# Memory keys and values inside the last attention head, sums of the normed x on VectorE, all gates in the pair stream

## The chip, the core and the metric

The kernel runs on one core of a Trainium2 chip. The core has TensorE (PE: matrix products, with a separate path for weight loads, PEld), VectorE (DVE), ScalarE (ACT), GpSimd (POOL) and SyncE (SP), each with its own instruction stream, and 16 DMA engines that move data between DRAM and the core's SBUF. The metric is the device time of one execution in microseconds (us); less is better. Three executions of the kernel before took 2409.5, 2413.11 and 2413.56 us; the median is 2413.11.

## The reference, cut to what matters

One layer of a streaming encoder runs on 1024 prompt tokens and 64 sample tokens (1088 in all), width 1024, in float32. One input projection makes the queries, keys and values of eight attention heads, the two inputs of a recurrent branch, the queries of a memory attention and three sets of gates. Beside it, 256 memory tokens are normed and turned into keys and values:

```python
def memory_kv(mem, g, wk, wv, k_norm_g):
    b, n, _ = mem.shape
    m = rms_norm(mem, g)
    k = rms_norm((m @ wk).reshape(b, n, MEM_HEADS, MEM_HEAD_DIM), k_norm_g)
    v = (m @ wv).reshape(b, n, MEM_HEADS, MEM_HEAD_DIM)
    return k.transpose(0, 2, 1, 3), v.transpose(0, 2, 1, 3)

def layer(x, past_k, past_v, conv_buf, h0, mem_k, mem_v, lw):
    xn = rms_norm(x, lw["norm_mix_g"])
    proj = xn @ lw["w_in"]
    # q_sb, k_sb, v_sb (8 heads x 128), x_lru, g_lru, q_mem (4 x 256), gates (3 x 1024)
    o_sb = stick_breaking_attention(q_sb, k_all, v_all, q_pos, k_pos)
    # o_lru: convolution, gated recurrence; o_mem: attention of q_mem over mem_k, mem_v
    g = jax.nn.sigmoid(gates + lw["b_merge"]).reshape(b, t, N_BRANCH, D_MODEL)
    merged = (g[:, :, 0] * (o_sb @ lw["w_br_sb"]) + g[:, :, 1] * (o_lru @ lw["w_br_lru"])
              + g[:, :, 2] * (o_mem @ lw["w_br_mem"]))
    x = x + merged @ lw["w_out"]
    # then a gated feed-forward block with its own norm
```

The memory keys and values of the prompt are outputs of the kernel and also operands of the memory attention, which comes much later.

## The kernel before, in words

**Products.** Every operand of a product is split into a high and a low half (`split`, L71 and L72: ScalarE casts the high half, VectorE or, where `l_eng=G` is given, GpSimd subtracts it to get the low half), and each product of tiles is three TensorE products (`mm3`, L99 to L101). Tokens lie along the free dimension in four chunks of 272. A weight of 1024 rows by 128 columns is loaded as one raw 128x1024 tile (three buffers, tag `raw`) and split into `wh` and `wl` (two buffers each); its load is issued on ScalarE's queue (L79).

**Stages in order.** The input is normed and transposed into operands B11, B12, B21, B22 (0 to about 40 us). Then come eight attention heads, then the memory keys and values (L791 to L842), then a stream of paired projections which fills the recurrent stage and the memory attention, then the branch outputs, the output projection and the feed-forward block.

**Fillers.** Attention alone does not fill TensorE: it waits for ScalarE and VectorE. So other products are issued between its parts. `Bulk` holds a generator; `bulk.run(n)` issues `n` steps of it at that place of the program. In the attention stage the generator is `bulk.steps(sb_stream())`: tile after tile of plain projections, three tiles (V, Q, K) for each head, each of 4 chunks x 8 steps, so 96 steps a head, one step three products of 128x272. While head `h` is computed, the tiles of head `h + 1` are issued. The last head has no next one; there the stream has four plain tiles of gates (`gate_tile`, `GATES_SB = 4`), 128 steps.

**The sums.** The later stream computes pairs of projections by seven products of sums of operands instead of eight products. It needs four sums per pair of row blocks: T3, T1, T2, T4, kept in DRAM. `x_sums` (L604 to L633) makes them from the normed x: 32 operations of 128x544 on GpSimd, in three buffers (`xq`). They are issued in a generator that the program advances between the steps of the heads; since nothing but the normed x is needed, most of them are done at the start.

**Order.** A scheduler (the tile framework) places each instruction by its place in the program and the priorities given; `high_priority` moves the emptying of a PSUM bank ahead. Each engine runs its own list in order. A buffer of a pool is reused when the last reader of its former content is done, and places in the pools of a later stage overlap those of an earlier one in SBUF: the pool `bt` (operands T2, T4, T1 of the stream and four spare places) lies where the attention pool `sb` was, while T3 lies in the places of B12.

**The memory section.** Two memory tiles are normed (L650), transposed in eight steps (L804) and scaled into `mTh` and `mTl`; then 16 halves (four heads, K and V, two halves each) of 8 x 3 products of 128x256 follow, each with its own weight; `mem_out` transposes the result back to tokens, norms the keys and stores. The key norm's factors are spread over the partitions by GpSimd (L796).

**The stream.** `pair_stream` (L738) issues 22 pairs, each seven operations of 24 products in 14 steps, 308 steps: 8 pairs of the recurrent inputs, 4 of the memory queries and 10 of the gates. The recurrent stage takes 14 + 8 x 23 of them, the memory attention 6 + 4 x 28; together that is 316, so the stream before runs out in the last memory head. If steps remain, they run by themselves behind it.

Of the kernel before, what the change touches and what calls it, by code (L numbers as in the profile page):

```python
# [2 lines left out]

# [6 lines left out]
F32 = mybir.dt.float32  # L10
# [7 lines left out]
P = 128  # L18
# [7 lines left out]
H = 8  # L26
# [22 lines left out]
def kernel(ctx: ExitStack, tc: tile.TileContext, x_prompt, x_sample, mem_prompt, cache_sb_k, cache_sb_v,  # L49
# [35 lines left out]
    GATES_SB = 4  # L85
# [183 lines left out]

    def gate_tile(b, f):  # L270

        def ev(ci, s, n, p):
            st = wpl.tile([P, HT], F32, tag="stg", name="gst", bufs=4)
            V.tensor_copy(st[:, :n], p)
            ST.dma_start(g_scr[b][f][:, s:s + n], st[:, :n])

        c0 = CGATE + b * D + f * P
        return (lambda: load_w(w_in[0, :, c0:c0 + P], f"wg{b}{f}", l_eng=G)), ev, []
# [39 lines left out]
    with ExitStack() as c1:  # L318
# [263 lines left out]
        heads, outs = {}, {}  # L582

        def sb_stream():
            tiles = []
            for h in range(H):
                tiles += sb_tiles(h)
            return tiles + [gate_tile(0, f) for f in range(GATES_SB)]

        bulk.gen = bulk.steps(sb_stream())  # L590
# [13 lines left out]
        def x_sums():  # L604

            for i in range(KT // 2):
                def quarter(k, half):
                    q = sb.tile([P, HT], F32, tag="xq", name=f"xq{k}{half}", bufs=3)
                    u = xq(k, half)
                    G.tensor_add(q, f32(u[:, 0]), f32(u[:, 1]))  # L610
                    return q
# [6 lines left out]
                G.tensor_sub(t3, t3, t1)  # L618
# [4 lines left out]
                G.tensor_sub(t1, t1, t2)  # L623
                ST.dma_start(s_scr[i]["T1"], t1)
                yield
                G.tensor_add(t2, t2, t3)
# [4 lines left out]
                G.tensor_sub(t4, t4, t2)  # L631
# [12 lines left out]
        mts = []  # L644
        for t in range(2):
            mt = o_tile(f"mt{t}")[:, :D]
            ST.dma_start(mt, mem_prompt[0, t * P:(t + 1) * P, :])
            junk = sb.tile([P, D], F32, tag=("ah", "al")[t], name="junk")
            S.activation(junk, mt, AF.Square, accum_out=ssx[:, t:t + 1])
            V.tensor_scalar(mt, mt, rstd(sb, ssx[:, t:t + 1], D, "rx"), None, op0=ALU.mult)  # L650
            mts.append(mt)
# [86 lines left out]
    def pair_stream(pairs, last):  # L738
# [14 lines left out]
        for i, (_, dst, _) in enumerate(pairs):  # L753
# [10 lines left out]
               f"wg{b}{j}_") for b in range(3) for j in range(NI) if b or 2 * j >= GATES_SB]  # L764

    with ExitStack() as c2:
# [23 lines left out]

        gkb = mk.tile([P, MHD], F32, name="gkb", bufs=1)
        gkr = mk.tile([1, MHD], F32, name="gkr", bufs=1)
        LD.dma_start(gkr, k_norm_g)
        G.partition_broadcast(gkb, gkr)  # L796
        mTh = mk.tile([P, KT, MEM], F32R, name="mTh", bufs=1)
        mTl = mk.tile([P, KT, MEM], F32R, name="mTl", bufs=1)

        def mem_norm():  # L800
            for k in range(KT):
                p = ps.tile([P, 512], F32, tag="gt", name="mtp", bufs=3)
                for t in range(2):
                    TE.transpose(p[:, t * P:(t + 1) * P], mts[t][:, k * P:(k + 1) * P], ident)  # L804
                gk = prm[:, PNE + k:PNE + k + 1]
                S.activation(mTh[:, k, :], p[:, :MEM], AF.Copy, scale=gk)
                V.scalar_tensor_tensor(mTl[:, k, :], p[:, :MEM], gk, f32(mTh[:, k, :]),
                                       op0=ALU.mult, op1=ALU.subtract)

        def mem_half(u, c, kf):  # L810

            c0 = (u // 2) * MHD + c * P
            wh, wl = load_w((w_mem_v if u % 2 else w_mem_k)[0, :, c0:c0 + P], f"wm{u}{c}")
            p = psm.tile([P, 512], F32, tag="mm", name="mmk")
            for k in range(KT):
                mm3(p[:, :MEM], wh[:, k, :], wl[:, k, :], mTh[:, k, :], mTl[:, k, :], k == 0, k == KT - 1)
            V.tensor_copy(kf[:, c, :], p[:, :MEM])

        def mem_out(u, kf):
            m, is_v = u // 2, u % 2  # L820
            p = ps.tile([P, 2, MHD], F32, tag="gt", name="mkt", bufs=3)
            for t in range(2):
                for c in range(2):
                    TE.transpose(p[:, t, c * P:(c + 1) * P], kf[:, c, t * P:(t + 1) * P], ident)
            ko = wpl.tile([P, HT], F32, tag="stg", name="ko", bufs=4)[:, :512].rearrange("p (t d) -> p t d", t=2)
            if is_v:
                V.tensor_copy(ko, p)
            else:
                ss = mk.tile([P, 2], F32, tag="ssk", name="ssk")
                for t in range(2):  # L830
                    S.activation(ko[:, t, :], p[:, t, :], AF.Square, accum_out=ss[:, t:t + 1])
                r = rstd(mk, ss, MHD, "rk")
                for t in range(2):
                    V.scalar_tensor_tensor(ko[:, t, :], p[:, t, :], r[:, t:t + 1], gkb, op0=ALU.mult, op1=ALU.mult)
            ST.dma_start((o_mv if is_v else o_mk)[0, 0, m].rearrange("(t p) d -> p t d", p=P), ko)

        mem_norm()
# [525 lines left out]
```

## Time and profile before

| | |
|---|---|
| runs | 2409.5, 2413.11, 2413.56 us; median 2413.11 |
| profiled execution | 2409.07 us, span 2407.3 us |
| TensorE busy | 2275.7 us of the span (95%), granted clock 0.981 |
| VectorE, ScalarE, GpSimd busy | 1613.1, 1204.9, 762.5 us |
| first score of head 0, of the last head | 88.32, 538.54 us |
| first memory transpose | 612.47 us |
| first product of the stream | 682.68 us |

The profile shows one execution. Its time of 2409.07 us is that of the whole execution, 1.8 us more than the span of the instructions. In rows of the stage view, an engine's busy time is followed by the number of its instructions in brackets. In rows of groups, `out<-in` are the names of tiles, then come shapes, the count, the busy time and the mean of one in ns, and behind the bar the idle time ahead of them with what ended most of it. In rows of single instructions the first two numbers are the start and the duration in us, and brackets at the end hold the idle time ahead with its releaser.

### The profile page before, as it was taken

The page shows a single profiled execution, that of the slowest core. Times are in us where ns is not written, and L with a number is a line of the kernel's source. Part 1 is how long each engine was busy: PE and PEld are TensorE (multiplying, and loading weights), DVE is VectorE, ACT ScalarE, POOL GpSimd, SP SyncE. Part 2 cuts the span into 40 slices and gives each one's busy share as a digit, 9 for nine tenths or more (in the row PEclk, how much of TensorE's full clock was granted, in tenths as well). Part 3 has the DMA queues.
Part 4 walks back from the last instruction along what each step waited for, and adds up shares of the span by engine and source line. Part 5 has one row for each costly group of instructions (what it writes and reads, how often), then busy time and mean ns, then how long its engine had stood idle before and what let it go on. Part 6 is the DMA issues. An engine that isn't in the chain of part 4 may idle for free.

```text
span 2407.3 us, 44757 instructions
## 1 busy us (share of the span) xinstructions
PE 2275.7 (95%) x17477; PEld 2210.0 (92%) x17477; DVE 1613.1 (67%) x2843; ACT 1204.9 (50%) x2449; POOL 762.5 (32%) x735
## 2 busy tenths in 40 slices
PE   6899999999899999999999999898999999999998
PEld 6788888888899999999999998888999999999998
DVE  4365656566767777766667758678766666677884
ACT  4355555555447565645566645466433333353553
POOL 5623232322002232111112265735334334340110
PEclk9899999999899999999999999999999999999999
DMA  4212121212744444434456645233223233263543
GB/s 158 89 51 76 53 76 51 68 42 94 224 132 139 142 156 149 140 124 129 132 185 215 221 128 193 78 121 102 95 86 109 95 100 101 86 219 117 172 138 88
DMA packets 329738, 293.26 MB, mean 122 GB/s; under 512 B 19491, under 2 KB 261366, under 8 KB 329526
## 3 DMA queue, kind: packets, MB, share of 16 engines
q1 hardware_dynamic: 283288, 267.26, 34.3%
q10 hardware_dynamic: 46238, 23.15, 3.3%
q8 instruction: 137, 2.24, 0.4%
q14 instruction: 75, 0.61, 0.1%
HBM read 194.34 MB, written 95.99 MB: 121 GB/s over the span
## 4 chain that ended last, share of the span: by engine, by line
PE 53%; DVE 9%; POOL 4%; DMA 4%; ACT 2%; issue 2%; SPq 0%; ACTq 0%; POOLq 0%; DVEq 0%
PE sw L192 46%; POOL swt L1129 1%; POOL mg L1133 1%; DMA sig<-g 1%; PE ssq L967 1%; DVE xc L872 1%; PE mmk L101 1%; DMA xT<-sT 1%; DVE x2T L72 1%; PE mmk L100 1%; PE mmk L99 1%; DVE x1T L72 0%; DVE h1T L72 0%; DVE xgT L72 0%; PE avm L99 0%
## 5 line engine op out<-in xcount | busy, mean ns | idle before, releaser
L202 ACT COPY swt<-sw 128x272 f32<-128x272 f32 x432 | 164.3, 385 | 217.1 <-PE sw L192 215.1
L1253 POOL TENSOR_TENSOR u<-u,R 128x272 f32<-128x272 f32 x66 | 65.8, 998 | 171.2 <-DVE u L1252 164.0
L462 DVE SCALAR_TENSOR_TENSOR e<-z,e 128x384 f32<-128x384 f32 (+4 forms) x96 | 51.1, 551 | 92.6 <-ACT e L460 92.3
L192 PE MATMUL sw<-xT,wg_S 128*128 128x272 f32 x720 | 101.6, 293 | 0.0
L192 PEld LDWEIGHTS sw<-xT,wg_S 128*128 128x128 f32 x720 | 94.8, 192 | 0.0
L463 DVE TENSOR_TENSOR_SCAN e<-ones,e 128x128 f32<-128x128 f32 (+3 forms) x64 | 92.4, 1451 | 0.6
L748 DVE TENSOR_TENSOR swt<-sw,swt 128x272 f32<-128x272 f32 x132 | 56.6, 434 | 49.5 <-PE sw L192 49.1
L1292 POOL TENSOR_TENSOR y<-y,swt 128x272 f32<-128x272 f32 x18 | 18.6, 1041 | 212.7 <-DVE swt L1291 211.7
L1262 ACT ACTIVATE sil<-sil 128x272 f32<-128x272 f32 x88 | 37.5, 429 | 80.1 <-POOL sil L1253 72.3
L192 PE MATMUL sw<-xT,wl_S 128*128 128x272 f32 x576 | 76.3, 289 | 0.0
L192 PEld LDWEIGHTS sw<-xT,wl_S 128*128 128x128 f32 x576 | 74.3, 189 | 0.0
L1269 DVE TENSOR_TENSOR u<-u,sil 128x272 f32<-128x272 f32 x88 | 39.3, 448 | 49.2 <-POOL u L1253 48.5
L467 ACT ACTIVATE e<-e 128x128 f32<-128x128 f32 (+3 forms) x64 | 43.8, 684 | 54.4 <-DVE e L466 38.8
L72 DVE TENSOR_TENSOR al<-at,ah 128x128 fp32r<-128x128 f32 (+2 forms) x96 | 51.2, 548 | 27.7 <-ACT ah L71 27.7
L1129 POOL TENSOR_TENSOR swt<-swt,sig 128x272 f32<-128x272 f32 x48 | 49.2, 1025 | 64.3 <-DVE swt L1128 64.3
L1253 POOL TENSOR_TENSOR sil<-sil,R 128x272 f32<-128x272 f32 x66 | 50.1, 780 | 60.4 <-DVE sil L1252 58.3
L192 PE MATMUL sw<-B,wg_A 128*128 128x272 f32 x480 | 68.1, 290 | 0.0
L245 POOL TENSOR_TENSOR ri<-ri,mhalf 128x2 f32<-128x2 f32 (+1 forms) x20 | 13.4, 672 | 167.0 <-DVE ri L244 150.0
L71 ACT CAST ah<-at 128x128 fp32r<-128x128 f32 (+2 forms) x96 | 44.2, 478 | 38.8 <-PE at L515 38.8
L192 PEld LDWEIGHTS sw<-B,wg_A 128*128 128x128 f32 x480 | 62.6, 188 | 0.0
L1133 POOL TENSOR_TENSOR mg<-mg,swt 128x272 f32<-128x272 f32 x64 | 60.8, 959 | 4.8 <-DVE swt L1131 1.0
L1122 ACT ACTIVATE sig<-sig,prm 128x544 f32<-128x544 f32 x48 | 35.2, 750 | 54.0 <-DMA sig<-g 46.0
(1523 smaller groups left out, 8139.6 us busy)
## 6 DMA issues: line engine op xcount, KB each, us to landing
sig<-g SPq DMA_DIRECT2D x48, 272.0 KB
hT<-u SPq DMA_DIRECT2D x44, 272.0 KB
g<-swt SPq DMA_DIRECT2D x40, 272.0 KB
wg_r<-in_w_in_dram SPq DMA_DIRECT2D x40, 256.0 KB
hB<-u SPq DMA_DIRECT2D x33, 272.0 KB
out_dram<-kvs SPq DMA_DIRECT2D x32, 256.0 KB
wl_r<-in_w_in_dram SPq DMA_DIRECT2D x32, 256.0 KB
sT<-xq SPq DMA_DIRECT2D x16, 272.0 KB
```

Of the source, the lines that this page charges most:

```text
L71: (h_eng or S.copy)(h, src)
L72: (l_eng or V).tensor_sub(l, src, f32(h))
L192: TE.matmul(bank[c][:, :HC], w[:, wj, i], x[:, xj, cs], start=start and i == 0 and j == 0, stop=i == n - 1 and j == 2, skip_group_check=True)
L202: S.copy(part(j, c), bank[c][:, :HC])
L462: V.scalar_tensor_tensor(ev, z, 0.0, ev, op0=ALU.max, op1=ALU.add)
L463: V.tensor_tensor_scan(e[:, ::-1], ones1[:n].to_broadcast([n, L]), e[:, ::-1], 0.0, op0=ALU.mult, op1=ALU.add)
L467: S.activation(e, e, AF.Exp)
L748: V.tensor_add(t, p, t)
L1129: G.tensor_mul(t if b else d, t, g)
L1133: G.tensor_add(d, d, t)
L1253: G.tensor_mul(d, d, r)
L1269: ffn_out(u, lambda f, hf, c, d: V.tensor_mul(d, d, sil[f][:, piece(hf, c)])), hswap=1)
```

## The change

Three things are changed together.

1. The 32 operations of `x_sums` run on VectorE in place of GpSimd.
2. The memory tiles are loaded and normed at the start of the last head, in buffers of the tag `raw`. The section for memory keys and values becomes a generator, `mem_steps`: 8 steps of transposing and scaling, then 16 halves of 8 steps, each three products of 128x256; 136 steps. It follows the projection tiles in the filler, so the last head is filled by it; what is left over runs behind the head. Its scaled operands lie in places of the keys and queries of the head before (`kh`, `kl`, `qh`, `ql`), its results in `kvf`, the norm factors in `pv`. The low halves of its weights are subtracted on GpSimd (`l_eng=G`), where VectorE did it before.
3. The four plain gate tiles are gone. The gates they made are two more pairs of the stream, which now has 24 pairs, 336 steps.

```diff
-    GATES_SB = 4
     HEAD_STEPS = 96
...
-    def gate_tile(b, f):
-
-        def ev(ci, s, n, p):
-            st = wpl.tile([P, HT], F32, tag="stg", name="gst", bufs=4)
-            V.tensor_copy(st[:, :n], p)
-            ST.dma_start(g_scr[b][f][:, s:s + n], st[:, :n])
-
-        c0 = CGATE + b * D + f * P
-        return (lambda: load_w(w_in[0, :, c0:c0 + P], f"wg{b}{f}", l_eng=G)), ev, []
...
+        def mem_load():
+
+            for t in range(2):
+                mt = wpl.tile([P, T], F32, tag="raw", name=f"mt{t}", bufs=RAWB)[:, :D]
+                ST.dma_start(mt, mem_prompt[0, t * P:(t + 1) * P, :])
...
+        def mem_out(u, kf, gkb):
...
+        def mem_steps():
+            mT = []
+            for x in "hl":
+                a = sb.tile([P, 1280], F32R, tag="k" + x, name=f"ma{x}")
+                b = sb.tile([P, T], F32R, tag="q" + x, name=f"mb{x}")
...
+            gk2 = sb.tile([P, 3, P], F32, tag="pv", name="gkb").rearrange("p a b -> p (a b)")
...
+            G.partition_broadcast(gkb, gkr[:1, :MHD])
+            for k in range(KT):
+                p = ps.tile([P, 512], F32, tag="tr", name="mtp", bufs=2)
+                for t in range(2):
+                    TE.transpose(p[:, t * P:(t + 1) * P], mts[t][:, k * P:(k + 1) * P], ident)
+                gk = prm[:, PNE + k:PNE + k + 1]
+                S.activation(mT[0][k], p[:, :MEM], AF.Copy, scale=gk)
+                V.scalar_tensor_tensor(mT[1][k], p[:, :MEM], gk, f32(mT[0][k]), op0=ALU.mult, op1=ALU.subtract)
+                yield
+            def weights(i):
+                u, c = i // 2, i % 2
+                c0 = (u // 2) * MHD + c * P
+                return load_w((w_mem_v if u % 2 else w_mem_k)[0, :, c0:c0 + P], f"wm{u}{c}", l_eng=G)
+            w = weights(0)
+            hook = None
+            for i in range(4 * MH):
+                u, c = i // 2, i % 2
+                wn = weights(i + 1) if i + 1 < 4 * MH else None
+                if c == 0:
+                    kf = sb.tile([P, 2, MEM], F32, tag="kvf", name=f"mf{u}")
+                p = psm.tile([P, 512], F32, tag="mm", name="mmk", bufs=2)
+                for k in range(KT):
+                    mm3(p[:, :MEM], w[0][:, k, :], w[1][:, k, :], mT[0][k], mT[1][k], k == 0, k == KT - 1)
+                    if k == 3 and hook:
+                        mem_out(*hook)
+                        hook = None
+                    if k == KT - 1:
+                        with tc.high_priority():
+                            V.tensor_copy(kf[:, c, :], p[:, :MEM])
+                    yield
+                if c:
+                    hook = u, kf, gkb
+                w = wn
+            mem_out(*hook)
...
-            return tiles + [gate_tile(0, f) for f in range(GATES_SB)]
-
-        bulk.gen = bulk.steps(sb_stream())
+            return tiles
+
+        bulk.gen = chain(bulk.steps(sb_stream()), mem_steps())
...
-                    G.tensor_add(q, f32(u[:, 0]), f32(u[:, 1]))
+                    V.tensor_add(q, f32(u[:, 0]), f32(u[:, 1]))
...
-                G.tensor_sub(t3, t3, t1)
+                V.tensor_sub(t3, t3, t1)
...
+            if h == H - 1:
+                mem_load()
             sb_attn(h)
...
-               f"wg{b}{j}_") for b in range(3) for j in range(NI) if b or 2 * j >= GATES_SB]
+               f"wg{b}{j}_") for b in range(3) for j in range(NI)]
...
-        mem_norm()
-        for u in range(2 * MH):
-            kf = mk.tile([P, 2, MEM], F32, tag="kf", name=f"mf{u}")
-            for c in range(2):
-                mem_half(u, c, kf)
-            mem_out(u, kf)
```

The order of instructions moves in three places. The first is GpSimd's list in the stage of the first head. `xq` are the sums, `wk0l` and `wv1l` are low halves of weights (K of head 0, V of head 1), `vl` and `kl` low halves of values and keys, `kvs` values in token order. Before:

```order
L610 TENSOR_TENSOR xq_3317<-B_87 128x544
L72 TENSOR_TENSOR wk0l<-wk0r,wk0h 128x1024
L623 TENSOR_TENSOR xq_2982<-xq_2982,xq_3317 128x544
L626 TENSOR_TENSOR xq_3317<-xq_3317,xq_2759 128x544
L610 TENSOR_TENSOR xq_3714<-B_95 128x544
L631 TENSOR_TENSOR xq_3714<-xq_3714,xq_3317 128x544
L72 TENSOR_TENSOR vl_507<-kvs,vh_506 128x512
L610 TENSOR_TENSOR xq_4060<-B_100 128x544
```

And changed:

```order
L422 MEMSET kh_1209 128x64
L423 MEMSET kl_1210 128x64
L73 TENSOR_TENSOR wk0l<-wk0r,wk0h 128x1024
L73 TENSOR_TENSOR vl_507<-kvs,vh_506 128x512 x2
L73 TENSOR_TENSOR wv1l<-wv1r,wv1h 128x1024
L73 TENSOR_TENSOR kl_627<-kf_625,kh_626 128x272 x3
L73 TENSOR_TENSOR wq1l<-wq1r,wq1h 128x1024
```

The sums have left the list, and the splits of weights, values and keys follow one another; on VectorE the sums now stand between the emptyings of V and Q (`vf<-mm`, `ql<-mm`).

The second place is SyncE's list where attention ends. `ko` are memory keys and values on their way out, `xT2..`, `xT4..`, `xT1..` and `xT3..` the stream's operands on their way in. Before:

```order
L722 DMA xT42_6933<-sT42_244 128x544
L722 DMA xT43_6937<-sT43_248 128x544
L722 DMA xT10_6941<-sT10_237 128x544
L722 DMA xT11_6945<-sT11_241 128x544
L722 DMA xT12_6949<-sT12_245 128x544
L722 DMA xT13_6953<-sT13_249 128x544
L157 DMA wl0_r1_7657<-in_w_in_dram 128x4x128 x2
L835 DMA out_6_dram<-ko_7110 128x2x256
L835 DMA out_7_dram<-ko_7190 128x2x256
```

And changed:

```order
L599 DMA out_7_dram<-ko_6943 128x2x256
L599 DMA out_6_dram<-ko_7016 128x2x256
L783 DMA xT20_7097<-sT20_235 128x544
L783 DMA xT21_7101<-sT21_239 128x544
L599 DMA out_7_dram<-ko_7070 128x2x256
L783 DMA xT22_7105<-sT22_243 128x544
L783 DMA xT23_7109<-sT23_247 128x544
L783 DMA xT40_7113<-sT40_236 128x544
L783 DMA xT41_7117<-sT41_240 128x544
L783 DMA xT42_7121<-sT42_244 128x544
```

The loads of T2, T4 and T1 stood ahead of every store of the memory section and stand now behind nearly all of them, since their places come free only when the memory work in the attention pool is done; the loads of T3 stay ahead.

The third place is GpSimd's list in the last head. `wg..l` and `wm..l` are low halves of gate and memory weights, `ah` and `al` blocks of attention weights that are set to zero, `gkb` the spread key norm, `rk` the root of a key's norm, `oh` the head's output. Before:

```order
L519 MEMSET ah 128x128
L520 MEMSET al 128x128
L72 TENSOR_TENSOR wg02l<-wg02r,wg02h 128x1024
L519 MEMSET ah 128x128
L520 MEMSET al 128x128
L296 TENSOR_TENSOR oh_6051<-oh_6051,oh_5325 128x544
L297 TENSOR_TENSOR oh_5325<-oh_5325 128x544
L298 TENSOR_TENSOR oh_5325<-oh_5325,oh_6051 128x544
L72 TENSOR_TENSOR wg03l<-wg03r,wg03h 128x1024
```

And changed:

```order
L613 ISA gkb<-gkr 128x256
L509 MEMSET ah 128x128
L510 MEMSET al 128x128
L73 ISA
L73 TENSOR_TENSOR wm10l<-wm10r,wm10h 128x1024
L73 TENSOR_TENSOR wm11l<-wm11r,wm11h 128x1024
L245 TENSOR_TENSOR rk<-rk,mhalf 128x2
L73 TENSOR_TENSOR wm20l<-wm20r,wm20h 128x1024
L73 TENSOR_TENSOR wm21l<-wm21r,wm21h 128x1024
L509 MEMSET ah 128x128
L510 MEMSET al 128x128
```

Where two splits of gate weights stood in this part of the list, four of memory weights stand now, and the spread of the key norm is among them, with an instruction of its own ahead of the next split.

More of the change, by code (lines that the diff above doesn't have):

```diff
@@ L2 @@
 from contextlib import ExitStack
+from itertools import chain
 import concourse.bass as bass
@@ L580, in sb_attn @@
                 put_branch(0, h // 2, outs.pop(h - 1), outs.pop(h))
-        heads, outs = {}, {}
+        def mem_load():
+            for t in range(2):
+                mt = wpl.tile([P, T], F32, tag="raw", name=f"mt{t}", bufs=RAWB)[:, :D]
+                ST.dma_start(mt, mem_prompt[0, t * P:(t + 1) * P, :])
+                junk = sb.tile([P, D], F32, tag=("ah", "al")[t], name="junk")
+                S.activation(junk, mt, AF.Square, accum_out=ssx[:, t:t + 1])
+                V.tensor_scalar(mt, mt, rstd(sb, ssx[:, t:t + 1], D, "rx"), None, op0=ALU.mult)
+                mts.append(mt)
@@ new lines, in mem_out @@
+        def mem_out(u, kf, gkb):
+            m, is_v = u // 2, u % 2
+            p = ps.tile([P, 2, MHD], F32, tag="tr", name="mkt", bufs=2)
+            for t in range(2):
+                for c in range(2):
+                    TE.transpose(p[:, t, c * P:(c + 1) * P], kf[:, c, t * P:(t + 1) * P], ident)
+            ko = wpl.tile([P, HT], F32, tag="stg", name="ko", bufs=4)[:, :512].rearrange("p (t d) -> p t d", t=2)
+            if is_v:
+                V.tensor_copy(ko, p)
+            else:
+                ss = sb.tile([P, 2], F32, tag="ssk", name="ssk")
+                for t in range(2):
+                    S.activation(ko[:, t, :], p[:, t, :], AF.Square, accum_out=ss[:, t:t + 1])
+                r = rstd(sb, ss, MHD, "rk")
+                for t in range(2):
+                    V.scalar_tensor_tensor(ko[:, t, :], p[:, t, :], r[:, t:t + 1], gkb, op0=ALU.mult, op1=ALU.mult)
+            ST.dma_start((o_mv if is_v else o_mk)[0, 0, m].rearrange("(t p) d -> p t d", p=P), ko)
@@ new lines, in mem_steps @@
+        def mem_steps():
[3 more added lines that the diff above has]
+                b = sb.tile([P, T], F32R, tag="q" + x, name=f"mb{x}")
+                mT.append([(a, b)[k // 5][:, k % 5 * MEM:(k % 5 + 1) * MEM] for k in range(KT)])
+            gk2 = sb.tile([P, 3, P], F32, tag="pv", name="gkb").rearrange("p a b -> p (a b)")
+            gkr = wpl.tile([P, HT], F32, tag="stg", name="gkr", bufs=4)
+            LD.dma_start(gkr[:1, :MHD], k_norm_g)
+            gkb = gk2[:, :MHD]
+            G.partition_broadcast(gkb, gkr[:1, :MHD])
+            for k in range(KT):
+                p = ps.tile([P, 512], F32, tag="tr", name="mtp", bufs=2)
+                for t in range(2):
+                    TE.transpose(p[:, t * P:(t + 1) * P], mts[t][:, k * P:(k + 1) * P], ident)
[28 more added lines that the diff above has]
+            mem_out(*hook)
@@ L584, in sb_stream @@
+        heads, outs, mts = {}, {}, []
         def sb_stream():
@@ L622, in x_sums @@
                 yield
-                G.tensor_sub(t1, t1, t2)
+                V.tensor_sub(t1, t1, t2)
                 ST.dma_start(s_scr[i]["T1"], t1)
                 yield
-                G.tensor_add(t2, t2, t3)
+                V.tensor_add(t2, t2, t3)
                 ST.dma_start(s_scr[i]["T2"], t2)
@@ L630, in x_sums @@
                 yield
-                G.tensor_sub(t4, t4, t2)
+                V.tensor_sub(t4, t4, t2)
                 ST.dma_start(s_scr[i]["T4"], t4)
@@ L642 @@
             pass
[L644 to L651, printed above, removed]
         bulk.run()
@@ L789 @@
         V.tensor_scalar(nclog, t1, -LRU_C, None, op0=ALU.mult)
[L793 to L822, printed above, removed]
-                for c in range(2):
[L824 to L835, printed above, removed]
@@ L837 @@
-        mem_norm()
-        for u in range(2 * MH):
-            kf = mk.tile([P, 2, MEM], F32, tag="kf", name=f"mf{u}")
-            for c in range(2):
-                mem_half(u, c, kf)
-            mem_out(u, kf)
     bulk.gen = pair_stream(pairs, lambda: pair_weights(w_br_sb, 0, "wb0", 1))
```

## The prediction

> **What bounds the kernel now.** I read the span by stages first, then the waits of the first stage, then the last attention head and what follows it. The columns of the stage view are the stretch, its length, the busy time (and instructions) of TensorE's products, its weight loads, VectorE, ScalarE and GpSimd, then the granted clock of TensorE, the DMA share and GB/s.
>
> ```profile
> 40.00:95.00 55.00, 42.30 (x296) 40.68 (x296) 9.21 (x21) 10.05 (x24) 53.32 (x44) 0.88 0.35 121
> 95.00:539.00 444.00, 421.20 (x3166) 389.95 (x3167) 269.96 (x472) 240.97 (x500) 138.31 (x149) 1.00 0.19 59
> 538.54:612.47 73.93, 69.98 (x534) 65.99 (x532) 42.33 (x73) 33.91 (x66) 19.26 (x17) 1.00 0.33 107
> 612.47:682.68 70.21, 59.72 (x440) 56.90 (x439) 52.36 (x105) 34.40 (x62) 4.26 (x5) 0.90 0.62 195
> 634.00:684.00 50.00, 48.52 (x386) 46.91 (x386) 33.82 (x54) 20.40 (x36) 4.12 (x8) 0.97 0.55 165
> 1860.00:1920.00 60.00, 60.00 (x483) 60.00 (x482) 39.92 (x64) 22.31 (x51) 28.56 (x26) 1.00 0.31 102
> ```
>
> TensorE is the bound almost everywhere: in a full stage 483 products of 128x272 take 60 us, 0.1242 us each. Two stretches stand out. In 40 to 95 us TensorE issues 296 products, worth 296 x 0.1242 = 36.8 us, in 55 us, while GpSimd is busy for 53.3. And the memory section, 612.5 to 682.7, is full only from 634 on: its first 21.5 us hold 59.72 - 48.52 = 11 us of products at most.
>
> The waits in the first stretch tell the chain:
>
> ```profile
> ACT kh L71 <- POOL wv1l L72: 14.7, 1, 14.7
> ACT vh L71 <- POOL wk0l L72: 8.5, 1, 8.5
> PE mm L99 <- DVE kf L443: 7.7, 1, 7.7
> PE mm L99 <- DVE ql L425: 4.0, 1, 4.0
> ```
>
> GpSimd's groups show what it did there, and below them stands one 128x1024 split of this stretch (wk0l) and one of the heads behind it (wv7l):
>
> ```profile
> L610 POOL TENSOR_TENSOR xq<-B 128x544 f32<-128x544 f32 x16 | 21.5, 1353 | 9.1 <-DVE B L368 8.5 <-DMA sT<-xq 0.4
> L618 POOL TENSOR_TENSOR xq<-xq,xq 128x544 f32<-128x544 f32 x4 | 5.4, 1356 | 0.2
> ...
> L72 POOL TENSOR_TENSOR wk0l<-wk0r,wk0h 128x1024 fp32r<-128x1024 f32 x1 | 2.4, 2351 | 0.0
> L72 POOL TENSOR_TENSOR wv7l<-wv7r,wv7h 128x1024 fp32r<-128x1024 f32 x1 | 4.4, 4376 | 0.0
> ```
>
> ScalarE issues the weight loads; a load waits for the raw buffer that a split on GpSimd still reads, and that split stands behind the sums. So ScalarE stands for 8.5 and 14.7 us, its casts of q and k come late, no PSUM bank is emptied, and TensorE stands for 4.0 and 7.7.
>
> **The sums.** 32 operations of 128x544 (16 of L610 and 4 each of L618, L623, L626, L631) leave GpSimd, 32 x 1.35 = 43 us, and go to VectorE. VectorE's nearest row is a difference of the same shape, beside ScalarE's cast of it:
>
> ```profile
> L72 DVE TENSOR_TENSOR xT<-xT 128x544 fp32r<-128x544 f32 x16 | 11.2, 719 | 0.9 <-ACT xT L71 0.8
> L71 ACT CAST xT<-xT 128x544 fp32r<-128x544 f32 x16 | 10.2, 645 | 4.5 <-DMA xT<-sT 4.4
> ```
>
> 32 x 0.72 = 23 us, on top of the 9.2 us that VectorE has in 55. Behind each sum stand the emptyings of q and k in VectorE's order; one or two sums ahead of one cost 0.7 to 1.5 us, and two banks with 24 products each (3 us) cover that. Three buffers serve the sums: a store of 272 KB took 2.8 us (row below), three sums take 2.2, so some sums wait 0.6 us for their buffer; also covered. The gain is bounded below by nothing, if VectorE takes GpSimd's part, and above by 55 - 36.8 = 18.2 us. The two waits of TensorE alone are 11.7; the products behind them ran at a lower clock (0.88 over the stretch). I take **-16 us**.
>
> The Trainium skill, GPSIMD Engine Reference (1. Specifications), says GpSimd's SBUF interfaces are shared with VectorE, with contention when VectorE reads two SBUF inputs; the sums do. The rows above, 2.35 us beside an idle VectorE and 4.38 in a busy head, agree. By that rule the splits left on GpSimd in this stretch would slow by up to 2 us each and the gain would be nearer -12.
>
> **The last head.** It loses the plain gate tiles, 4 x 4 x 24 = 384 products, 384 x 0.1242 = 47.7 us, and keeps 73.9 - 47.7 = 26.2 us of its own attention. It gets 384 memory products of 128x256 and 48 transposes: 432 instructions. From the stage 634 to 684 one takes 48.52 / 386 = 0.1257 us: 54.3 us. The place where the section now ends and the first score of heads 0 and 7 are these:
>
> ```profile
> 88.32 0.27 ACT L458 ACTIVATE e<-z 128x128 f32<-128x128 f32 x1
> ...
> 538.54 0.27 ACT L458 ACTIVATE e<-z 128x128 f32<-128x128 f32 x1
> ...
> 682.68 17.41 PE sw L192 x139
> ```
>
> New waits come with it. (a) The eight norm steps carry two transposes each where a step had three products; TensorE has little to fill the first scores with. (b) A gate weight served 96 products (12 us); a memory weight serves 24 (3 us), so 16 loads, casts and splits fall into one head instead of four, and the low half is now split on GpSimd, 2.35 to 4.38 us against 1.23 on VectorE before:
>
> ```profile
> 673.39 1.23 DVE L72 TENSOR_TENSOR wm70l<-wm70r,wm70h 128x1024 fp32r<-128x1024 f32 x1 [0.54 <-ACT wm70h L71]
> ...
> 565.28 0.37 ACTq L79 DMA_DIRECT2D wm01r<-in_w_mem_k_dram  x1
> 565.70 0.85 ACT L467 ACTIVATE e<-e 128x768 f32<-128x768 f32 x1 [4.10 <-POOL al L520]
> ...
> 587.98 0.37 ACTq L79 DMA_DIRECT2D wm10r<-in_w_mem_v_dram  x1
> 588.40 1.06 ACT L467 ACTIVATE e<-e 128x1024 f32<-128x1024 f32 x1 [6.78 <-POOL al L520]
> ...
> 617.68 0.55 POOL L796 PARTITION_BROADCAST gkb<-gkr  x1 [6.21 <-ACT mTh L806]
> ```
>
> (c) GpSimd also makes the broadcast of the key norm, which had 6.2 us of idle ahead of it, and the sums of the last head pair. Nothing of this costs anything while attention's products cover it (the gates' loads stopped ScalarE for 4.1 and 6.8 us and TensorE lost little). Where attention is over, about the last six halves, one place of a weight takes cast 1.05 + split 2.35 + 24 products 3.0, 6.4 us for two places, 3.2 a half against 3.0. Bounds: 0, and 25 (each half pays half of the 4.38 - 1.23 = 3.15 us by which its split grew, 16 x 1.6). I take **10**: 4 in the norm steps, 4 in the middle, 2 behind attention.
>
> **Behind the section.** The operands T2, T4 and T1 of the stream lie where attention's buffers were. Twelve loads of 272 KB now start only when the last memory transposes have read their tile; before, they ran beneath the section:
>
> ```profile
> 612.42 2.76 DMA xT<-sT
> ...
> 615.20 0.64 ACT L71 CAST xT<-xT 128x544 fp32r<-128x544 f32 x1 [2.31 <-DMA xT<-sT]
> ...
> 630.27 0.64 ACT L71 CAST xT<-xT 128x544 fp32r<-128x544 f32 x1
> ```
>
> Sixteen came in 15.1 us, 1.0 each, after 2.8. A piece is ready 2.8 + 0.65 + 0.72 = 4.2 us after its issue, the fourth T2 at about 7.2 + 1 (transposes) = 8.2, the fourth T4 at 12.2, the fourth T1 at 16.2. Each of the first two products of the stream (B11, and T3, which lies in a free place and is early) takes 24 x 0.1242 = 3 us. The fourth pieces are wanted at 7.1, and behind each wait 3 us later: TensorE waits 1.1 + 1 + 1 = **3 us** (0 to 10, the whole of the twelve loads less the six covered).
>
> **The gates in the stream.** Two pairs of 14 steps, 336 products x 0.1242 = **41.7 us**; they lengthen the stream to 336 steps, the 316 of the LRU and memory attention take what they took, and 20 run by themselves at the full rate. 40 to 43 bound it: 28 more bank copies and sums ride beneath products as in the other pairs.
>
> **The sum.** From the first score of the last head to the stream: before 682.7 - 538.5 = 144.1 us; now 26.2 + 54.3 + 10 + 3 + 41.7 = 135.2, so -8.9. With the sums, -24.9. The profiled execution took 2409.1 us: 2384.2. The median of the runs, 2413.1, is 4 us above it: **2388 us**.
>
> **Rivals.** (1) *The splits on GpSimd set the pace of the last head*: the 25 us above in place of 10, 2403. For it: 4.38 us for a split in a busy head; against it: GpSimd was busy for 19.3 of 73.9 us there. (2) *VectorE takes GpSimd's part in the first stretch*: the sums wait for buffers and hold up q and k; no gain of 16, 2404. Against it: 23 + 9.2 us of 55. (3) *ScalarE stops at each memory load*, on the other side: 14 loads at the mean of 4.10 and 6.78, 5.4 us, with TensorE standing each time because too few products are queued: 76 us in place of 10, 2454. It decides from 35 / 14 = 2.5 us per load on; below, the kernel is still faster. Against it: the raw buffers are free earlier once the memory rows have been read. (4) *The work is only moved*: TensorE is full in both places and waits wherever it waited; then only 48 products fewer, 6 us, are gained and the new waits eat them: 2413.
>
> **How the numbers follow.** Forecast 0.56, rival 1 0.15, rival 2 0.12, rival 3 0.11, rival 4 0.06. The range 2370 to 2408 holds the forecast with the bounds of its costs (all covers hold: 18.2 for the sums, no new waits, -40) and rivals 1 and 2; rivals 3 and 4 and part of the others' tails are left out. About 0.2% (5 us) is what a measurement can tell: faster 0.83, same 0.06, slower 0.11.
>
> **What would show it.** Right: the first score of head 0 near 72 us in place of 88.3, no wait of ScalarE over 4 us for GpSimd before 95 us, products near 42 us busy in a stretch of 40; the last head's first score to the first stream product about 90 us; waits of a few us for T2, T4, T1; no plain section behind the head. Wrong: TensorE waiting for a split (wm..l) in every half, for sums on VectorE in the first stretch, or a stream that ends later than the memory attention by more than 30 us.

## The result and the profile after

The changed kernel takes 2395.39 us (median of 5 runs, 2391.85 to 2401.57), the kernel before 2412.09 (median of 5). The ratio is 0.9939, with a 95% interval of 0.9919 to 0.9958: about 15 us faster (0.0061 x 2410), where 25 had been forecast. The profiled execution of the change took 2398.64 us, span 2396.9, 10.4 us less than that of before.

Both traces can be cut at the same marks. For the change, the stage view (columns as before) is:

```profile
40.00:95.00 55.00, 50.41 (x387) 47.77 (x386) 45.79 (x73) 19.13 (x42) 14.52 (x14) 1.00 0.42 141
78.10:524.94 446.84, 423.91 (x3191) 392.54 (x3191) 274.66 (x482) 245.75 (x511) 141.57 (x153) 1.00 0.20 61
524.94:621.25 96.31, 79.53 (x578) 72.81 (x576) 57.84 (x97) 50.32 (x101) 51.35 (x32) 0.93 0.43 131
621.25:984.60 363.35, 342.98 (x2629) 339.44 (x2628) 274.04 (x424) 219.18 (x372) 91.30 (x81) 0.99 0.47 152
984.60:1370.70 386.10, 384.66 (x3058) 377.19 (x3058) 253.36 (x570) 217.08 (x483) 60.09 (x61) 1.00 0.50 162
1701.00:2141.00 440.00, 440.00 (x3501) 439.60 (x3501) 289.07 (x490) 169.39 (x375) 183.35 (x171) 1.00 0.33 108
```

and the same stretches of the kernel before, from the first score of head 0 on:

```profile
88.32:538.54 450.22, 426.61 (x3206) 394.71 (x3205) 271.89 (x476) 242.42 (x505) 144.46 (x155) 1.00 0.19 59
538.54:681.50 142.96, 128.52 (x963) 121.84 (x961) 93.77 (x175) 67.17 (x125) 23.52 (x22) 0.95 0.47 150
681.50:1039.70 358.20, 341.09 (x2623) 338.31 (x2622) 263.37 (x381) 212.15 (x358) 91.95 (x81) 0.99 0.45 145
1039.70:1385.70 346.00, 344.13 (x2725) 336.77 (x2725) 234.06 (x536) 195.79 (x446) 58.79 (x60) 1.00 0.52 168
1715.00:2152.00 437.00, 437.00 (x3501) 436.79 (x3500) 289.25 (x490) 169.19 (x374) 182.51 (x171) 1.00 0.34 109
```

| stretch | before | after | difference |
|---|---|---|---|
| start to the first score of head 0 | 88.32 | 78.10 | -10.2 |
| first score of head 0 to that of the last head | 450.22 | 446.84 | -3.4 |
| first score of the last head to the stream | 142.96 | 96.31 | -46.7 |
| stream to the first memory attention | 358.20 | 363.35 | +5.2 |
| memory attention and gates, to the branches | 346.00 | 386.10 | +40.1 |

To the branches this is -15.0 us, of which -13.6 stand there already when the last head begins. What follows, -46.7 + 5.2 + 40.1, is -1.4: of all the moving of memory work and gates nearly nothing is left. The other 4.6 us between -15.0 and -10.4 come mostly in the feed-forward part, which the change does not touch: the last row of each fence has 3501 products, in 440 us here and 437 before, so these products ran 0.7% slower in that execution; no trace here shows why.

### The profile page after: what moved, and what is told of

It is laid out like the page before. It is cut to its first block, busy times and chain, and to the rows that moved or that the text cites. A ratio compares the mean times of both kernels' runs of the same rounds, so it can differ in the third digit from the quotient of the medians.

```text
span 2396.9 us, 44723 instructions
## 1 busy us (share of the span) xinstructions
PE 2267.3 (95%) x17429; PEld 2200.5 (92%) x17429; DVE 1635.7 (68%) x2877; ACT 1221.6 (51%) x2481; POOL 750.6 (31%) x715
## 4 chain that ended last, share of the span: by engine, by line
PE 52%; DVE 9%; POOL 5%; DMA 4%; issue 4%; ACT 2%; SPq 0%; ACTq 0%; POOLq 0%; DVEq 0%
PE sw L192 46%; POOL swt L1137 1%; DMA sig<-g 1%; POOL mg L1141 1%; DVE xc L880 1%; PE ssq L975 1%; PE avm L99 0%; DVE x2T L73 0%; DVE h0T L73 0%; DVE x1T L73 0%; DVE xgT L73 0%; PE gt L99 0%; DMA o1B<-gl 0%; PE sc L101 0%; PE sc L100 0%
## 5 line engine op out<-in xcount | busy, mean ns | idle before, releaser
L192 PE MATMUL sw<-xT,wg_S 128*128 128x272 f32 x864 | 119.4, 290 | 0.0
L192 PEld LDWEIGHTS sw<-xT,wg_S 128*128 128x128 f32 x864 | 111.5, 188 | 0.0
L809 DVE TENSOR_TENSOR swt<-sw,swt 128x272 f32<-128x272 f32 x144 | 61.7, 434 | 46.0 <-PE sw L192 45.3
L192 PE MATMUL sw<-B,wg_A 128*128 128x272 f32 x576 | 81.0, 290 | 0.0
L192 PEld LDWEIGHTS sw<-B,wg_A 128*128 128x128 f32 x576 | 75.0, 188 | 0.0
```

The costliest lines, as they stand in the source:

```text
L192: TE.matmul(bank[c][:, :HC], w[:, wj, i], x[:, xj, cs], start=start and i == 0 and j == 0, stop=i == n - 1 and j == 2, skip_group_check=True)
L809: V.tensor_add(t, p, t)
```

## The experiments

Ratios are to the kernel before in runs on the same chip. The runs were made on several chips, so two changed kernels are compared by their ratios; differences in us are worked out with 2410.

### Each part alone

The kernel before with the sums moved (five lines `G.tensor_add`, `G.tensor_sub` of `x_sums` to `V`), and the change with them moved back:

```diff
# sums alone, in the kernel before
-                    G.tensor_add(q, f32(u[:, 0]), f32(u[:, 1]))
+                    V.tensor_add(q, f32(u[:, 0]), f32(u[:, 1]))
...
# memory and gates alone, in the change
-                    V.tensor_add(q, f32(u[:, 0]), f32(u[:, 1]))
+                    G.tensor_add(q, f32(u[:, 0]), f32(u[:, 1]))
```

> The kernel before with one part of the change alone: the 32 sums on VectorE. Theory A (the profiles of before and of the change differ by 13.6 us at the first score of the last head, and by 15.0 at the first gated product of the branches, so the sums gave nearly all of it and the memory work only moved its waits): 13 to 15 us below before, so no more than 2 us above the whole change. Theory B (both parts of the forecast's sum worked, each somewhat smaller): 10 us below before or less, and 5 us or more above the whole change. In the trace the first score of head 0 is near 78 us either way.

> The change with the sums back on GpSimd: memory keys and values in the last head and all gates in the stream, alone. Theory A: within 3 us of before (46.6 us won from the first score of the last head to the stream, 45.2 lost behind it). Theory B: 5 to 9 us below before.

The sums alone: 2399.17 us, 0.9951 (0.9939 to 0.9964), -11.8 us. Memory and gates alone: 2409.44, 1.0002 (0.9993 to 1.0011), nothing. The second is theory A without doubt; the first lies between the two theories, 2.9 us above the whole change, and its interval reaches both. Moving the memory work and the gates, as it is made in this change, is worth 0 to 3 us.

### What the last head waits for

In the last head of the change, the largest waits of TensorE are these (releaser behind the arrow: total, times, longest). `mtp` are the memory transposes, `mmk` the memory products, `mal` the low half of their operand, `z` attention's scores, `e` its weights in the making; further down, `at` are transposes of these weights, `av` their products with the values, `kvt` transposes of values, and `mm` plain projections.

```profile
PE mmk L101 <- POOL wm40l L73: 4.8, 1, 4.8
PE mmk L101 <- POOL wm10l L73: 1.9, 1, 1.9
PE mmk L99 <- ACT wm10h L72: 1.7, 1, 1.7
PE mtp L617 <- DVE mal L620: 1.4, 1, 1.4
PE z L99 <- DVE e L456: 1.2, 1, 1.2
PE mmk L101 <- POOL wm20l L73: 1.0, 1, 1.0
PE mmk L101 <- POOL wm30l L73: 1.0, 1, 1.0
```

Low halves of weights on GpSimd lead. GpSimd's list shows two of these at work:

```profile
534.72 0.55 POOL L613 PARTITION_BROADCAST gkb<-gkr  x1 [6.18 <-PE mtp L617]
...
544.61 2.34 POOL L73 TENSOR_TENSOR wm10l<-wm10r,wm10h 128x1024 fp32r<-128x1024 f32 x1 [9.03 <-ACT e L450]
...
578.12 1.36 POOL L286 TENSOR_TENSOR oh<-oh,oh 128x544 f32<-128x544 f32 x1 [3.24 <-DMA o0B<-oh]
579.56 1.35 POOL L287 TENSOR_TENSOR oh<-oh 128x544 f32<-128x544 f32 x1
580.99 3.21 POOL L288 TENSOR_TENSOR oh<-oh,oh 128x544 f32<-128x544 f32 x1
584.14 2.74 POOL L73 TENSOR_TENSOR wm40l<-wm40r,wm40h 128x1024 fp32r<-128x1024 f32 x1
```

`wm40l` stands behind the three sums of the head pair; ScalarE had made its high half by 580.78. `wm10l` starts at 544.61, though ScalarE had made its high half by then:

```profile
540.84 1.05 ACT L72 CAST wm10h<-wm10r 128x1024 fp32r<-128x1024 f32 x1
```

That is 2.7 us after 541.89. VectorE did nothing from 542.42 to 544.64, so it did not hold the split up; the only instruction between the zeroing of `al` and the split on GpSimd is the one that follows a broadcast. Two experiments, each one edit of the change:

```diff
# low halves on VectorE
-                return load_w((...)[0, :, c0:c0 + P], f"wm{u}{c}", l_eng=G)
+                return load_w((...)[0, :, c0:c0 + P], f"wm{u}{c}")
...
# key norm's factors spread by their transfer
-            LD.dma_start(gkr[:1, :MHD], k_norm_g)
-            G.partition_broadcast(gkb, gkr[:1, :MHD])
+            LD.dma_start(gkb, k_norm_g[0].partition_broadcast(P))
```

> The change with the low halves of the memory weights on VectorE in place of GpSimd. Theory A1 (GpSimd's order of work is what is late in the last head: TensorE waits there for low halves on GpSimd 1.90, 1.02, 0.99, 4.77, 0.49 and 0.54 us, 9.7 us in all, and runs at a clock of 0.5 behind two of these waits): the waits for wm..l vanish, the last head takes 85 to 90 us from its first score to the stream in place of 96.3, and the kernel is 7 to 11 us faster than the change. Theory A2 (VectorE, busy for 51.6 of the first 87 us, takes the lateness over): the waits go by VectorE's name and the time is within 3 us of the change, or longer.

> The change with the key norm's factors spread over the partitions by the transfer that loads them, so that GpSimd has neither the broadcast nor the instruction that follows it. GpSimd idled for 9.0 us between the broadcast and the split wm10l, and wm10l began 2.7 us after TensorE had taken up wm10h. Theory A1: the split of wm10l starts with its cast, TensorE's wait of 1.90 us and the 5 us at half clock behind it go: 3 to 5 us faster than the change. Theory A2 (the cast of wm10h on ScalarE, for which TensorE waited 1.73 us, is as late): 0 to 1.5 us.

> The change with both edits: low halves of the memory weights on VectorE, and the key norm's factors spread by their transfer. Theory C (the broadcast cost what it cost because splits of weights were queued behind it on GpSimd; with the splits on VectorE nothing of weight stands behind it): within 2 us of the kernel with the splits on VectorE alone. Theory D (two causes of their own, 6.8 and 5 us): 4 us or more below that kernel.

Low halves on VectorE: 2389.98 us, 0.9911 (0.9898 to 0.9925), 6.7 us below the change. The broadcast gone: 2391.16, 0.9918 (0.9905 to 0.9932), 5.1 below. The intervals of both touch that of the change (0.9919 to 0.9958), so these two sizes are rough. Both: 2390.33, 0.9919 (0.9904 to 0.9933), no more than one of them: theory C. The broadcast cost something because splits were queued behind it on GpSimd: in four traces with the broadcast ahead of it (the change, memory and gates alone, and the change with late sums on either engine, below) `wm10l` started 7.8 to 9.0 us after the last operation on GpSimd, and 0.6 to 2.7 us after its cast; without the broadcast it started 0.1 us after its cast. In the three profiles the stretch from the first score of the last head to the stream is 88.48, 90.75 and 85.73 us in place of 96.31. With the low halves on VectorE, one wait kept its size and changed its releaser:

```profile
PE mmk L101 <- DVE wm40l L73: 5.0, 1, 5.0
```

So theory A1 holds for the time, at the lower end of what it said, and A2 for this one wait: the split that stood behind sums on GpSimd stands behind scans on VectorE.

### Memory weights first, and halves on both engines

```diff
# memory weights first
-                return load_w(...)
+                with tc.high_priority():
+                    return load_w(...)
...
# first half-tile on GpSimd, second on VectorE (with late sums, below)
+                ... f"wm{u}{c}", l_eng=None if c else G)
```

> As the one with both edits, and the casts and splits of the memory weights go ahead of everything else that is ready on ScalarE and VectorE. Theory E (TensorE's longest wait that was left with the splits on VectorE, 5.0 us for wm40l, comes from a scan of 2.3 and other attention work standing ahead of the split): that wait goes, 3 to 6 us faster than the one with both edits. Theory F (the memory products then run earlier, and attention's chain is late by what was put ahead of it and without cover at its end): 0 to 5 us slower.

> As the kernel with all three edits, but the low half of every first memory half-tile on GpSimd and of every second on VectorE. The wait of 5.0 us for wm40l, which stayed when all low halves were on VectorE, had the split behind a scan of 2.3 us. If the queue on VectorE makes that wait, it falls to 2 us or less and the kernel is 2 to 5 us faster than with all on VectorE; if the late cast on ScalarE or the order of the scores makes it, or scans beside GpSimd's splits take longer (3.98 us against 2.05), it is the same within 2 us or slower.

Weights first: 2392.32 us, 0.9932 (0.992 to 0.9945), against 0.9919 for the same kernel without; the intervals overlap, no gain, theory F rather than E. The wait for `wm40l` is gone, and the stretch is longer all the same, 88.61 us against 85.73, with the waits on attention's side:

```profile
PE z L99 <- DVE e L456: 3.2, 5, 2.2
PE mmk L101 <- DVE wm60l L73: 1.9, 1, 1.9
PE at L505 <- DVE al L73: 1.6, 2, 0.9
```

Halves on both engines: 2382.87 us, 0.9902 (0.9881 to 0.9922), 10 us slower than with all on VectorE (0.986, last experiment). Its wait for `wm40l` is gone too; instead TensorE waits for the end of attention's chain, by the lists of TensorE and of VectorE:

```profile
575.30 0.69 PE L507 MATMUL at<-ident,e 128*128 128x128 f32 x2 [6.92 <-ACT e L459]
```

```profile
568.12 3.12 DVE L455 TENSOR_TENSOR_SCAN e<-ones,e 128x1024 f32<-128x1024 f32 x1
571.16 1.75 DVE L455 TENSOR_TENSOR_SCAN es<-ones,es 64x256 f32<-64x256 f32 x1
```

With all halves on GpSimd, all on VectorE and some on each, one long wait (4.8, 5.0 and 6.9 us) is left at the same place, where the longest scores of the head are made. With the weights first the longest is 2.2, and the stretch is no shorter for it.

### The last head without a filler

```diff
-        bulk.gen = chain(bulk.steps(sb_stream()), mem_steps())
+        bulk.gen = bulk.steps(sb_stream())
...
+        bulk.gen = mem_steps()
         bulk.run()
```

> The change with the memory steps behind the last head in place of in it; the gates stay in the stream. This is the last head without a filler. By the forecast's sum attention alone would take 26.2 us of TensorE and the memory work 54.3 + up to 25: 105 us or less from the last head's first score to the stream. Theory I (attention without a filler is set by the chain from scores through ScalarE and VectorE, whose busy times in the head are some 34 and 42 us): the head alone takes 45 to 60 us, and with the memory work behind it the stretch is 110 to 125 us in place of 96.3; the kernel is 15 to 28 us slower than the change.

2418.04 us, 1.0039 (1.0025 to 1.0053), 24 us slower than the change: theory I. The head by itself and the memory work by itself:

```profile
524.43:580.03 55.60, 29.14 (x144) 22.90 (x143) 34.23 (x53) 28.66 (x60) 9.07 (x13) 0.75 0.17 55
580.03:643.74 63.71, 57.59 (x434) 53.75 (x434) 22.25 (x44) 23.27 (x42) 37.92 (x19) 0.95 0.50 150
```

Attention alone takes 55.6 us with 29.1 of TensorE in it: its chain through ScalarE and VectorE sets it, as TensorE's two largest waits there say, 12.6 us for `e` on VectorE and 9.9 for `e` on ScalarE. Filling it with the memory work saves 119.3 - 96.3 = 23 us; before, the gates filled it, and the memory work took its time alone. Only one of the two can be the filler, so the move gives one cover up for another. That it came out even is not settled by this alone: with its splits in another place the same move wins (see "All together").

### The place of the sums

```diff
+                mark[0] = V.tensor_sub(ev, z, ev)
...
-                    next(sums, None)
+                    with tc.issue_after(mark[0].ins):
+                        next(sums, None)
```

The scheduler issues the sums in the first stretch, as soon as they are ready. This edit queues each behind attention work of the heads: in the change on VectorE; in the change on GpSimd (behind its zeroing of `al`); and on VectorE in the kernel before.

> The change with the sums kept on VectorE, but each queued there behind attention work of heads 1 to 7 in place of the first stretch. Theory G (in 55 to 75 us the sums stand ahead of the emptying of q, VectorE is busy for 4.9 to 5.0 us of each 5, and TensorE waits 3.0 us for ql): the first score of head 0 comes at about 74 us in place of 78.1, and the kernel is 3 to 4 us faster than the change. Theory H (32 sums of 0.7 to 1.4 us lengthen VectorE's chain in the heads by as much as they leave the first stretch): first score early, but the last head's first score no earlier than 524.9, and no gain.

> The change with the sums back on GpSimd, but there late, queued behind work of heads 1 to 7. Theory K (the sums cost time through their place ahead of weights, keys and queries in the first stretch, whatever their engine): first score of head 0 at 72 to 75 us and within 3 us of the same kernel with late sums on VectorE. Theory L (the engine matters: one sum takes 1.35 us on GpSimd and stands ahead of splits of weights, keys and values there, and the splits of VectorE slow beside it): first score as early, but heads that are longer, last head's first score at 520 us or later, 5 us or more above the kernel with late sums on VectorE.

> The kernel before with the sums on VectorE and late, and nothing else of the change. By theory A (the memory work inside the last head only moves its waits, with 0 to 3 us to either side) it is within 4 us of the change with late sums: a ratio to before of 0.988 to 0.991. If the memory work inside the head is worth more beside a VectorE without early sums, the ratio is 0.992 or more.

Late on VectorE: 2381.43 us, 0.9894 (0.9874 to 0.9913), 10.8 us below the change, more than theory G's 3 to 4, since the heads became shorter as well. Late on GpSimd: 2395.03, 0.9942 (0.9926 to 0.9958), as good as early on VectorE, and 11.6 above late on VectorE: theory L. Late on VectorE in the kernel before: 2382.64, 0.9899 (0.9877 to 0.9921), theory A once more, since the rest of the change adds 1 us to it; the two intervals would allow some 7 to either side.

In the first stretch of the change VectorE was busy for 45.79 of 55 us (first fence above) and all but full from 50 to 65, and one wait of VectorE and the largest of TensorE there were these:

```profile
DVE xq L678 <- DMA sT<-xq: 3.4, 2, 1.8
...
PE mm L99 <- DVE ql L415: 3.0, 3, 1.7
```

With the sums late on VectorE the stretch is full, and the heads are shorter, 441.61 us against 446.84:

```profile
40.00:95.00 55.00, 54.80 (x420) 52.45 (x421) 22.72 (x46) 23.14 (x50) 13.66 (x14) 0.99 0.21 60
72.60:514.21 441.61, 424.55 (x3204) 394.78 (x3203) 291.16 (x512) 247.93 (x511) 132.68 (x153) 1.00 0.22 71
```

With them late on GpSimd the first stretch is as full, but the heads are long:

```profile
40.00:95.00 55.00, 54.84 (x425) 52.59 (x425) 23.28 (x47) 23.60 (x50) 13.61 (x14) 1.00 0.21 60
72.03:524.81 452.78, 425.73 (x3204) 393.83 (x3203) 280.29 (x482) 246.01 (x510) 185.20 (x185) 1.00 0.22 70
```

The waits of TensorE in the heads (95 to 514 us) name where. Late on VectorE, then late on GpSimd:

```profile
PE z L99 <- DVE e L458: 5.7, 7, 0.8
PE at L507 <- DVE al L73: 2.5, 7, 0.5
...
PE kvt L377 <- DVE al L73: 1.2, 5, 0.6
```

```profile
PE kvt L377 <- DVE al L73: 9.5, 10, 1.1
PE av L99 <- ACT ah L72: 4.9, 7, 0.7
PE mm L99 <- DVE ql L415: 4.6, 7, 1.2
```

In the change, with the sums early, these three are 4.5, 4.9 and 4.7 us. Work on VectorE that is held up beside GpSimd's sums fits the 9.5: scans of 128x896 in the heads took 2.48 us on average with the sums late on GpSimd against 2.01, and those of 128x384 1.36 against 0.95. That the other two vanish with the sums on VectorE is a matter of order: TensorE's list in the heads is another one there (the values' transposes and the last scores stand in other places among the filler steps). Which of these changes in order brings the 5.2 us in the heads was not taken apart.

### All together

The change with late sums on VectorE, low halves on VectorE and no broadcast:

> The change with what helped so far: sums late in the heads, low halves of the memory weights on VectorE, key norm's factors spread by their transfer. If the two gains lie in different stages (the sums' 10.8 us ahead of the last head's first score, the splits' 6.8 behind it), they add: about 17 us below the change, 2374 to 2379. If VectorE, which then carries both, is late in the last head: 2380 or more.

2374.88 us, 0.986 (0.9841 to 0.9879): 19 us below the change and 34 below the kernel before, as expected. It is the fastest here; a wait of 5.2 us for `wm40l` is still in it.

This run also prices the move of the memory work and the gates anew. The kernel before with late sums (0.9899, same chip) differs from this one by that move alone, now with its low halves on VectorE and without the broadcast: 0.0039 x 2410 = 9 us, though the two intervals just touch. With early sums it is as much, 0.9951 for the sums alone against 0.9911 with the move and its low halves on VectorE, and there the intervals lie apart. The stretch from the first score of the last head to the stream, in the kernel before with late sums and in this one:

```profile
514.34:655.85 141.51, 127.59 (x962) 121.62 (x961) 94.47 (x177) 66.89 (x125) 22.64 (x22) 0.95 0.48 153
514.89:600.82 85.93, 76.75 (x578) 71.13 (x576) 67.89 (x114) 50.50 (x101) 10.95 (x16) 0.94 0.50 153
```

Here 55.6 us are won, against some 45 lost behind it (the +5.2 and +40.1 of the table). So the move does win by itself. The change lost most of that where the splits of its weights waited on GpSimd, behind the broadcast and other work: either edit, low halves on VectorE or no broadcast, brings 5 to 7 us back.

## Why the prediction came out as it did

The side and the range held, and of 25 us about 15 came. The mechanism held for the sums; of the 8.9 us forecast for the memory work and the gates 1.4 came, and the range still held because it was wide enough to take in rivals 1 and 2. Term by term, against the profiled execution:

- **The sums, -16.** Measured -13.6 at the first score of the last head, -11.8 alone. Removing them from GpSimd did what was said: no wait of ScalarE over 4 us for a split on GpSimd is left, and the two waits of 7.7 and 4.0 us fell to 0.2 and 3.0. The sign "near 72 us" did not come: the first score of head 0 stood at 78.10, and only late sums brought it to 72.60. What failed is the sentence that one or two sums ahead of an emptying are covered by two banks: VectorE's queue was full from 50 to 65 us, three or four sums stood between two emptyings of Q, and TensorE waited 3.0 us for Q. The sums were also longer than priced, 28.1 us in all where 23 had been put, because VectorE had to wait for splits on GpSimd (last section):

```profile
L686 DVE TENSOR_TENSOR xq<-xq,xq 128x544 f32<-128x544 f32 x4 | 5.7, 1420 | 0.0
...
60.99 2.62 POOL L73 TENSOR_TENSOR wv1l<-wv1r,wv1h 128x1024 fp32r<-128x1024 f32 x1 [5.28 <-ACT wv1h L72]
```

  The one sum of L686 that started at 61.41, beside this split, took 2.80 us in place of 0.72. The prediction had looked for this on the other side, up to 2 us on each split; the three weight splits of the stretch took 2.39 to 2.63, against 2.34 to 2.38 before. The wait for buffers was 3.4 us, more than the 0.6 given (its row of 2.8 us is a load, `xT<-sT`, and not a store), but TensorE was busy for 5.00 and 4.76 of the 5 us around its two parts. The bound of "18.2 above" held for the change but looked at the first stretch alone: late sums won 24.3 us up to the last head (538.54 - 514.21), since the heads became shorter too.
- **The last head, 90.5 us (26.2 + 54.3 + 10).** Measured 96.3: by the forecast's own terms the new waits are 15.8, not 10. "4 in the middle" was the step that was too small: the waits there by name are `wm40l` 4.8, `wm20l` and `wm30l` 1.0 each, and the two for `wm10` 3.6, and behind `wm10l` and `wm40l` TensorE ran at half its clock (0.50 from 545 to 550 us, and last section). The cause was named, rival 1's price of 25 was too high. With the low halves on VectorE the stretch is 88.48, so about 8 of the 15.8 came from having them on GpSimd. The norm steps show one wait of 1.4 us, less than the 4 given for them.
- **26.2 us of attention's own.** As TensorE work it is near (29.1 busy alone, at a granted clock of 0.75), as time it is not: alone the head takes 55.6. Neither filler shows it, since both cover it.
- **T2, T4 and T1, 3 us.** The trace has one wait of 0.46 us for them. The rest of the +5.2 from the stream to the memory attention is in the recurrent stage, where TensorE waited 13.0 us for `xh` against 9.4:

```profile
PE gt L99 <- ACT xh L72: 13.0, 5, 3.6
...
PE sw L192 <- ACT xT L72: 0.5, 1, 0.5
```

  In six traces with the memory work and the gates moved that wait is 11.1 to 13.0 us, and 9.4 to 9.6 in the three without. So the longer wait goes with the move; whether the twelve loads beside that stage's own make `xh` late was not tried.
- **The gates, +41.7.** Measured +40.1, within the bounds given.
- **The start of the last stretch.** The forecast counted the section before to 682.7; the first product of the stream stands at 681.48, so 1.2 us of its gain were not there.

Of the rivals, the fourth ("the work is only moved") was given 0.06 as a whole; for the memory half of the change its number came, and only the sums kept the kernel faster. Its reason did not quite: the same move wins 9 us with its splits on VectorE, so most of what ate the gain is rival 1's cause, splits that come late from GpSimd. Rival 2 was half right: VectorE was full in the first stretch, at a price of some 3 us there and not 16. Rival 3 (ScalarE stopping at each load) came in part: ScalarE stood for 5.1 us around the load of `wm40r`, 5.6 around that of `wm51r`, 3.0 around `wm71r` and 2.1 around `wm41r`, each issued as the split of an earlier tile (`wm21l`, `wm40l`, `wm60l`, `wm30l`) ended on GpSimd. Over 14 loads that is 1.1 us each, below the 2.5 from which it was to decide.

## What to carry to other kernels

A filler is worth what it covers. A move of work into the place of another filler is priced by what the chain takes alone (here 55.6 us with 29.1 us of TensorE work), by what becomes of the old filler, and by whether the new one gets its operands in time: the same move was worth 0 to 3 us with its weight splits on GpSimd behind a broadcast, and about 9 with them on VectorE. When work leaves a crowded engine, its place in time matters as much as its engine: the same sums on VectorE were worth 12 us early and 24 late, and late on GpSimd 14. And taking one named wait away need not shorten a stretch: each choice of engine for the splits moved the long wait to a new name, and with the weights first it was gone and the stretch was 2.9 us longer (88.61 against 85.73).

## What the hardware showed

**A scan on VectorE and a subtraction or sum on GpSimd blocked each other for the whole instruction.** In the last head of the change, a split on GpSimd and a scan on VectorE:

```profile
568.44 2.38 POOL L73 TENSOR_TENSOR wm30l<-wm30r,wm30h 128x1024 fp32r<-128x1024 f32 x1 [5.16 <-issue]
...
568.71 3.98 DVE L453 TENSOR_TENSOR_SCAN e<-ones,e 128x896 f32<-128x896 f32 x1
```

The same scan with GpSimd idle, in the kernel with the low halves on VectorE:

```profile
565.65 2.01 DVE L453 TENSOR_TENSOR_SCAN e<-ones,e 128x896 f32<-128x896 f32 x1
```

The split ran from 568.44 to 570.82; 570.82 + 2.01 = 572.83, and the scan ended at 572.69. The scan's time is as if it had not run slower but begun when the split was done. The other way round, the third sum of the head pair took 3.21 us where its neighbours took 1.36, beside a scan of 2.34 us that started 0.27 ahead of it. Not every operation of VectorE is held up: beside the same split `al<-at,ah`, which reads `at` from PSUM, took 0.29 us, and 0.28 with GpSimd idle. The Trainium skill, SBUF — State Buffer (SBUF: two separate sides), says of the ports that the two engines share that, of a VectorE operation with two SBUF inputs and a GpSimd operation that reads SBUF, whichever starts first holds them for its whole instruction and the other blocks; these rows agree.

**The clock fell after a wait of 4.8 us, and that cost half as much again.** Two stretches of 5 us behind the wait for `wm40l` in the change (columns as in the stage view; the clock is third from the end):

```profile
587.00:592.00 5.00, 5.00 (x24) 5.00 (x25) 0.50 (x1) 1.54 (x3) 3.03 (x3) 0.51 0.51 157
592.00:597.00 5.00, 5.00 (x45) 5.00 (x45) 3.29 (x7) 2.63 (x5) 2.55 (x2) 1.00 0.43 130
```

TensorE was busy all through both, and issued 24 instructions in the first and 45 in the second: by this estimate 5 x (1 - 24 / 45) = 2.3 us were lost on top of the wait. The Trainium skill, TensorE: Matmul & The Clock Gate (Part 1: The HAM clock gate), has the array fall to half its clock after an idle window of about 3.4 us and return after one that is busy. The granted clock agrees: TensorE stopped at 582.17, the clock was 1.00 until 585 and 0.50 from 586 on, and the 5 us for which it stayed low under work are one to two such windows.
